# Interleaving two float32 tensors: eight equal tiles in place of seven and a shrinking tail

## The chip, the core and the metric

The kernel runs on one NeuronCore of one Trainium2 chip. The number that counts is the device time of one execution in microseconds (us), as the median of repeated runs. Beside it there is a profile of one execution, whose span runs from the first to the last instruction on the core and is therefore a little shorter than the device time.

## What is computed

Two inputs of the same shape are woven together element by element. Nothing is added or multiplied; every input element is read once and written once.

```python
batch, seq, dim = 32, 256, 1024
x, y: float32 [batch, seq, dim]

result = np.zeros((batch, seq, dim * 2), dtype=np.float32)
result[..., 0::2] = x
result[..., 1::2] = y
```

Each input has 8,388,608 elements, which is 33.55 MB. The kernel reads 67.11 MB and writes 67.11 MB.

## The kernel before

The tensors are taken as flat arrays. Spread over 128 partitions, each input is 65,536 elements for every partition. This is cut into tiles of `lw` elements per partition. A tile is one contiguous stretch of memory, and partition p holds its p-th row of `lw` elements. A full tile (`WL` = 8192) has rows of 32 KiB and is 4 MiB for x and 4 MiB for y.

```python
P = 128
WL = 8192
WS = 4096

xpool = ctx.enter_context(tc.tile_pool(name="xp", bufs=2))
ypool = ctx.enter_context(tc.tile_pool(name="yp", bufs=2))
opool = ctx.enter_context(tc.tile_pool(name="op", bufs=2))

lwidths = [WL] * (total // P // WL - 1) + [4096, 2048, 1024, 512, 512]

start = 0
for lw in lwidths:
    xtile = xpool.tile([P, WL], fp32, name="xtile")[:, :lw]
    ytile = ypool.tile([P, WL], fp32, name="ytile")[:, :lw]
    # ... xs, ys: 128 rows of lw elements, from element `start` on
    nc.sync.dma_start(out=xtile, in_=xs)                              # L49
    nc.sync.dma_start(out=ytile, in_=ys)                              # L50

    soff = 0
    while soff < lw:
        width = min(WS, lw - soff)
        otile = opool.tile([P, 2 * WS], fp32, name="otile")[:, : 2 * width]
        # ... os_: 128 rows of 2*width elements, 2*lw apart
        nc.vector.tensor_copy(out=otile[:, 0::2], in_=xsub)           # L63
        nc.vector.tensor_copy(out=otile[:, 1::2], in_=ysub)           # L64
        nc.scalar.dma_start(out=os_, in_=otile)                       # L65
        soff += width
    start += P * lw
```

Three engines take part. SyncE issues all loads on one DMA queue (q1 in the profile). VectorE (DVE) copies x into the even and y into the odd columns of an output tile. ScalarE (ACT) issues all stores on another DMA queue (q10).

A full tile is worked in two halves of 4096 elements. Each half gives one store of 128 rows of 32 KiB, so 4 MiB. In the text, "store (6,1)" means the second half of tile 6, where tiles are counted from 0. The tail consists of tiles of 4096, 2048, 1024, 512 and 512 elements, each worked in a single piece.

There are two buffers each for x tiles, y tiles and output tiles. Three waits follow from this:

- A load of tile i+2 is issued when the copies of tile i have read their buffer.
- The first copy of a half (L63) needs its x tile, and the output buffer of two halves earlier must have been stored.
- The second copy of a half (L64) needs its y tile.

Of the kernel before, what the change touches and what calls it, by code (L numbers as in the profile page):

```python
# [2 lines left out]

# [4 lines left out]


@with_exitstack
def kernel(
    ctx: ExitStack,
    tc: tile.TileContext,
    x: bass.AP,
    y: bass.AP,
    out: bass.AP,
):
    nc = tc.nc
    P = 128  # L20

    total = 1
    for s in x.shape:
        total *= s

    WL = 8192
    WS = 4096

    xf = x.rearrange("b s d -> (b s d)")
    yf = y.rearrange("b s d -> (b s d)")  # L30
    of = out.rearrange("b s d -> (b s d)")

    fp32 = mybir.dt.float32

    xpool = ctx.enter_context(tc.tile_pool(name="xp", bufs=2))
    ypool = ctx.enter_context(tc.tile_pool(name="yp", bufs=2))
    opool = ctx.enter_context(tc.tile_pool(name="op", bufs=2))

    lwidths = [WL] * (total // P // WL - 1) + [4096, 2048, 1024, 512, 512]
    assert sum(lwidths) == total // P  # L40

    start = 0
# [4 lines that stand above are left out]
        xs = dataclasses.replace(xf, offset=start, ap=[[lw, P], [1, lw]])  # L47
        ys = dataclasses.replace(yf, offset=start, ap=[[lw, P], [1, lw]])
# [7 lines that stand above are left out]
            os_ = dataclasses.replace(  # L56
                of,
                offset=2 * start + 2 * soff,
                ap=[[2 * lw, P], [1, 2 * width]],
            )  # L60
            xsub = xtile[:, soff : soff + width]
            ysub = ytile[:, soff : soff + width]
# [6 lines that stand above are left out]
    assert start == total  # L69


# [1 line left out]
_INS = ['x', 'y']  # L73
_OUTS = [((32, 256, 2048), 'float32')]


# [23 lines left out]
```

## Time and profile before

| quantity | value |
|---|---|
| device time, median of 3 runs | 318.54 us (318.42 to 318.84) |
| span of the profiled execution | 316.3 us |
| VectorE busy | 73.5 us, 38 copies |
| one copy of 128x4096 | 2.29 us (x30) |
| copies of 128x2048, 128x1024, 128x512 | 1.23, 0.70, 0.43 us (x2, x2, x4) |
| loads / stores issued | 24 / 19 |
| load of a full x tile, a full y tile, issue to landing (median) | 42.0, 59.2 us |
| store of 4 MiB, issue to landing (median) | 30.6 us |

The profile's page gives the busy time of each engine, the activity over 40 slices of the span, the traffic of the two DMA queues, and the chain of work that ended last. A transfer's time from issue to landing includes the time that it stands in its queue behind earlier transfers and the time in which the sixteen DMA engines serve the other queue. It is not what one transfer takes by itself. "Share" of the DMA is the mean busy share of the core's sixteen DMA engines. A transfer is made of packets, which the profile assigns to a window by their start; here a packet is one row of a tile, and there are also 4-byte packets that signal completion.

### The profile page before, as it was taken

How to read it: one execution, taken by the hardware profiler on the slowest of the kernel's cores; microseconds unless marked ns; L12 is line 12 of the kernel's file. 1: busy time of each engine (PE TensorE's matmuls, PEld its weight loads, DVE VectorE, ACT ScalarE, POOL GpSimd, SP SyncE). 2: the span in 40 equal slices, each digit the busy share in tenths (PEclk: the TensorE clock that was granted, in tenths of full speed). 3: DMA queues.
4: the chain of work that ended last, by engine and by line, in shares of the span. 5: the costliest groups of instructions: out<-in, count | busy, mean ns of one | idle time of the engine just before them, and what ended most of it. 6: DMA issues, size and time to landing. Idle time of an engine off the chain costs nothing.

```text
span 316.3 us, 179 instructions
## 1 busy us (share of the span) xinstructions
DVE 73.5 (23%) x38; POOL 0.2 (0%) x4
## 2 busy tenths in 40 slices
DVE  0334002214022220313205040050501414221022
POOL 0000000000000000000000000000000000000000
DMA  8999999999999999999999999999999999999997
GB/s 332 406 456 394 427 435 439 423 448 414 456 410 456 406 456 406 460 423 439 435 427 443 419 452 410 456 410 456 406 456 406 460 431 423 435 435 415 414 395 305
DMA packets 6192, 134.22 MB, mean 424 GB/s; under 512 B 688, under 2 KB 688, under 8 KB 1712
## 3 DMA queue, kind: packets, MB, share of 16 engines
q1 hardware_dynamic: 3456, 67.11, 49.9%
q10 hardware_dynamic: 2736, 67.11, 49.2%
HBM read 67.11 MB, written 67.11 MB: 424 GB/s over the span
## 4 chain that ended last, share of the span: by engine, by line
DMA 89%; DVE 10%; issue 0%; SPq 0%; DVEq 0%
DMA out_dram<-otile 59%; DMA ytile<-in_y_dram 29%; DVE otile L64 6%; DVE otile L63 4%; SPq L49 0%; DVEq L63 0%
## 5 line engine op out<-in xcount | busy, mean ns | idle before, releaser
L63 DVE COPY otile<-xtile 128x4096 f32<-128x4096 f32 (+3 forms) x19 | 37.1, 1958 | 203.7 <-DMA out_dram<-otile 180.6
L64 DVE COPY otile<-ytile 128x4096 f32<-128x4096 f32 (+3 forms) x19 | 37.1, 1956 | 35.5 <-DMA ytile<-in_y_dram 35.5
L84 POOL MEMSET const-bfloat16-1.0<- 128x1 bf16 x1 | 0.1, 103 | 0.0
L84 POOL MEMSET const-uint8-127<- 128x1 uint8 x1 | 0.1, 102 | 0.0
L84 POOL MEMSET const-float32-0.0<- 128x1 f32 x1 | 0.1, 99 | 0.2 <-issue 0.2
L84 POOL MEMSET const-float32-1.0<- 128x1 f32 x1 | 0.1, 99 | 0.0
## 6 DMA issues: line engine op xcount, KB each, us to landing
out_dram<-otile ACTq DMA_DIRECT2D x15, 4096.0 KB, 30.6
xtile<-in_x_dram SPq DMA_DIRECT2D x7, 4096.0 KB, 42.0
ytile<-in_y_dram SPq DMA_DIRECT2D x7, 4096.0 KB, 59.2
xtile<-in_x_dram SPq DMA_DIRECT2D x1, 2048.0 KB, 37.2
ytile<-in_y_dram SPq DMA_DIRECT2D x1, 2048.0 KB, 49.5
out_dram<-otile ACTq DMA_DIRECT2D x1, 2048.0 KB, 7.7
xtile<-in_x_dram SPq DMA_DIRECT2D x1, 1024.0 KB, 28.8
ytile<-in_y_dram SPq DMA_DIRECT2D x1, 1024.0 KB, 35.4
```

Source lines behind the costliest of these rows:

```text
L63: nc.vector.tensor_copy(out=otile[:, 0::2], in_=xsub)
L64: nc.vector.tensor_copy(out=otile[:, 1::2], in_=ysub)
L84: nc = _bacc.Bacc("TRN2", target_bir_lowering=False, num_devices=1)
```

## The change

The five tiles of decreasing size at the end are replaced by one more full tile. The total is the same 65,536 elements for each partition. All loads and all stores then are 4 MiB with rows of 32 KiB. There are 16 loads in place of 24, 16 stores in place of 19, and 32 copies in place of 38; everything up to the first seven tiles is issued in the same order. The purpose is a plainer kernel with only large transfers. What is given up is the gradual end, in which the last load, the last copies and the last store are all small.

```diff
--- before.py
+++ after.py
@@ -36,7 +36,7 @@
     ypool = ctx.enter_context(tc.tile_pool(name="yp", bufs=2))
     opool = ctx.enter_context(tc.tile_pool(name="op", bufs=2))
 
-    lwidths = [WL] * (total // P // WL - 1) + [4096, 2048, 1024, 512, 512]
+    lwidths = [WL] * (total // P // WL)
     assert sum(lwidths) == total // P
 
     start = 0
```

## The prediction

> **What bounds the kernel now.** I read first the page's slices and queue totals, then the stretches table by stage, then the DMA view of single windows, and last the timeline around the end. The page, with the busy tenths and the rates in the 40 slices:
>
> ```profile
> DVE 73.5 (23%) x38; POOL 0.2 (0%) x4
> ...
> DMA  8999999999999999999999999999999999999997
> GB/s 332 406 456 394 427 435 439 423 448 414 456 410 456 406 456 406 460 423 439 435 427 443 419 452 410 456 410 456 406 456 406 460 431 423 435 435 415 414 395 305
> ```
>
> VectorE works a quarter of the span. The DMA engines are full in every slice but the first and the last. The chain of waits gives 89% to DMA, but which transfer it names is of little use: both queues share the same sixteen engines, so a wait on a store is also a wait on loads. The kernel is a queue of 134.2 MB for a saturated resource. Only what keeps that resource idle, or makes it less efficient, costs time. The stretches by stage show where that is (duration, DVE busy, POOL busy, clock, DMA share, GB/s):
>
> ```profile
> 25.00:249.75 224.75, 50.02 (x23) 0.00 (x0) 1.00 1.00 431
> 249.75:301.00 51.25, 13.79 (x7) 0.00 (x0) 1.00 1.00 429
> 301.00:312.00 11.00, 2.30 (x6) 0.00 (x0) 1.00 0.98 397
> 312.00:316.30 4.30, 0.73 (x2) 0.00 (x0) 1.00 0.54 221
> ```
>
> Share 1.00 up to 301 us, through the body and the first tail tile; then 397 GB/s, and 221 in the last stretch. So a change of the tail can act only on the last 15 us, and, where packets are smaller, slightly before. The steady state is periodic; here is one period of the timeline (start, duration, operation, idle before and its releaser):
>
> ```profile
> 205.38 2.30 DVE L63 COPY otile<-xtile 128x4096 f32<-128x4096 f32 x1 [14.85 <-DMA out_dram<-otile]
> ...
> 211.03 2.30 DVE L64 COPY otile<-ytile 128x4096 f32<-128x4096 f32 x1 [3.35 <-DMA ytile<-in_y_dram]
> ...
> 224.75 2.30 DVE L63 COPY otile<-xtile 128x4096 f32<-128x4096 f32 x1 [11.43 <-DMA out_dram<-otile]
> ...
> 244.11 2.29 DVE L63 COPY otile<-xtile 128x4096 f32<-128x4096 f32 x1 [14.86 <-DMA out_dram<-otile]
> ...
> 249.75 2.30 DVE L64 COPY otile<-ytile 128x4096 f32<-128x4096 f32 x1 [3.35 <-DMA ytile<-in_y_dram]
> ```
>
> A tile takes 249.75 - 211.03 = 38.72 us and moves 16 MiB = 16.777 MB, so the full rate is 16.777 / 38.72 = 433.3 GB/s. That is the yardstick below. At 249.75 us tile 6's y has landed; what follows in the old kernel is the changed part.
>
> **What the Trainium skill says.** (1) "DMA: Bandwidth & Descriptors", section "Queues, rings and completion order": each DMA engine takes turns between the queues it has work for, a packet at a time. The trace agrees. With 32 KiB rows on both sides (100 to 138.7 us) the two queues have 50.2% and 50.0%; with stores of 32 KiB rows against loads of 16 KiB rows and less, the stores get two thirds (249.75 to 301 us):
>
> ```profile
> DMA packets 1343, 21.97 MB, mean 429 GB/s; under 512 B 144, under 2 KB 144, under 8 KB 383
> ## 3 DMA queue, kind: packets, MB, share of 16 engines
> q10 hardware_dynamic: 513, 14.71, 66.5%
> q1 hardware_dynamic: 830, 7.25, 33.4%
> ```
>
> (2) The same page, "Measured (HBM→SBUF, 128 partitions, SWDGE, issued from GpSimd)", asks for transfers of 1 MiB or more for 75% of the peak. The old tail has transfers of 256 and 512 KiB. The trace has them beside other transfers, and so loses much less: 397 GB/s from 301 to 312 us. (3) "HBM Reference", section "Specifications (TRN2)": 358 GB/s is a core's share of the memory, and a core alone gets about 425. The steady state here is 433.3, so the share does not bind in the mix of reads and writes. Whether it does when only writes are left is the rival below.
>
> **The change part by part.** The old tail has ten loads, five stores (the first of 4 MiB) and ten copies (two of them full-sized); the new tile has two loads, two stores and four copies, all full-sized. In VectorE time: out go 2 x 1.23 + 2 x 0.70 + 4 x 0.43 = 5.6 us, in come 2 x 2.29 = 4.6 us. None of that counts by itself, since VectorE idles beside full DMA engines.
>
> *Cost of the old tail.* From 249.75 to 301 us 21.97 MB were moved in 51.25 us; at 433.3 it would be 50.70, so 0.5 us is lost to smaller packets. From 301 us on, the DMA view counts 5.31 MB, which is 12.25 us of full rate. The last store is issued at 312.7 us (end of the last copy) and lands 2.6 us later, at 315.3 us, so 14.3 us pass: 2.0 us lost to short packets and to the end's waits (the two last 512-wide pieces each wait for a store before them: 5.79 and 2.29 us on VectorE). Together 2.5 us is all that the change can give.
>
> *New end by bytes.* After 249.75 us 21.97 + 5.31 = 27.28 MB remain to be started, and sixteen 32 KiB packets are under way, on average half done: 0.26 MB. At 433.3 GB/s, 27.54 MB take 63.6 us: 313.3 us as the mean end of the sixteen engines. They do not end together: the trace's completion records of tile 6's y run from 248.5 to 249.4 us. Taking 0.6 us for the last one beyond the mean gives a last landing at 313.9 us.
>
> *New end by the chain.* This asks whether the store queue ever runs dry. Tile 7's y copy starts one period after tile 6's, at 249.75 + 38.72 = 288.5 us. Store (6,0) lands for the copy at 244.11 + 38.72 = 282.8; store (6,1) would at 302.2 if loads still took every other turn. From 288.5 on there are none, and the remaining 13.7 us halve to 6.9: 295.4 us. Store (7,0) is issued when its y copy ends, 288.5 + 2.3 = 290.8, which is 4.6 us before (6,1) is through, so the queue does not run dry. A 4 MiB transfer alone takes 9.7 us (the first y lands 22.78 - 13.09 = 9.69 us after the first x, with nothing else running): 305.1 us. Store (7,1) needs the buffer of (6,1), free at 295.4, and two copies (4.5 us with their overlap): issued at 299.9, 5.2 us ahead. It lands at 305.1 + 9.7 = 314.8, less the 0.4 us that the copies' starts lie behind the landings: 314.4 us.
>
> The two ways give 313.9 and 314.4. In the old kernel the span ends 316.3 - 315.3 = 1.0 us after the last landing. So the new span is 314.9 to 315.4 us, 1.2 us under the old one in the middle; the time is 318.54 - 1.2 = 317.3 us, or 0.4% less.
>
> **The rivals.** *The exposed end.* The ordinary argument for shrinking tiles: after the last load lands, the old kernel has 316.3 - 308.9 = about 7 us left, the new one 315 - 288.5 = 26.5 us with nothing beside it but stores; one would fear up to 20 us. Against it: the bytes are the same, loads merely finish 20 us sooner because they get half of the turns to the end, where the old tail gave stores two thirds. As long as the store queue is full, nothing is lost. It would come true only if one of the two margins (4.6, 5.2 us) vanished; a dry spell costs at most 2 to 5 us: 319 to 322 us.
>
> *Stores alone are slower than the mix.* The last 26 us would be pure writing, a state the old trace nearly lacks. If writes got only the skill's 358 GB/s, (6,1)'s rest, (7,0) and (7,1), which is 26.3 us at 433.3, would take an estimated 31.8: +5.5 us, 322.8 us. Against it speaks the one stretch in which stores have the engines nearly to themselves, 304 to 308 us:
>
> ```profile
> DMA packets 192, 1.74 MB, mean 434 GB/s; under 512 B 16, under 2 KB 16, under 8 KB 96
> ## 3 DMA queue, kind: packets, MB, share of 16 engines
> q10 hardware_dynamic: 96, 1.57, 91.8%
> q1 hardware_dynamic: 96, 0.16, 10.7%
> ```
>
> Nine tenths stores at 434 GB/s. Loads alone (4 to 22 us, 99.5% of the engines' time on q1) move 430. I take it that one engine's pace on a packet is the limit, whatever the direction.
>
> *Nothing at all.* A last large store leaves the engines to finish apart, and the loss at the end replaces that of small packets: 318.0 to 318.6 us.
>
> **Range and chances.** 2.5 us is the most that can be won (316.0), and half of it is expected. The skew of the engines can take another 0.6 us or give it back. A somewhat slower pure store phase (5%) would add 1.3 us, which makes the range longer upwards: 316.6 to 318.8 us. A 2% gain (312.2) is out of reach, since the bytes at full rate forbid it: 0.01. A 2% loss (324.9) needs stores alone to be slower by a quarter: 0.03. Within 2%: 0.96.
>
> **What the changed profile should show.** The y copy of tile 7 at 288.5 us; the copy that waits for store (6,1) at 295.4, and thus the last store issued near 299.9; DMA share 1.00 from 25 us to about 313; a rate of 430 or more from 290 to 312 with q10 alone; last landing at 313.9 to 314.4; span near 315.1. I am wrong if the pure store stretch shows under 420 GB/s (second rival), or the share falls between 290 and 312 us (first), or the share is full and the span still no shorter (third).

## The result, and the profile after

The new kernel takes 316.74 us (median of 4 runs, 316.72 to 317.46) against 318.69 us of the old one beside it (4 runs). The ratio is 0.9939, with a 95% interval of 0.9914 to 0.9964. Run again in a later series it has 317.09 us and a ratio of 0.9940 (0.9928 to 0.9953). Predicted were 317.3 us and a range of 316.6 to 318.8, so the time lies close to the lower end. The span of the profiled execution is 315.0 us; 316.3 us was the old one, 314.9 to 315.4 the forecast.

The page of the new kernel, with the busy tenths and the rates in 40 slices:

```profile
DVE 72.6 (23%) x32; POOL 0.2 (0%) x4
...
DMA  8999999999999999999999999999999999999997
GB/s 333 408 458 387 412 454 412 454 412 454 412 454 412 458 408 458 408 458 408 458 408 458 424 441 424 441 429 437 429 437 429 437 429 437 433 433 437 429 437 304
```

The old kernel's rate fell over its last three slices (395 and 305 in the last two). Now only the last slice falls. The same stretches as before, from the table by stage (duration, DVE busy, POOL busy, clock, DMA share, GB/s):

```profile
25.00:249.75 224.75, 49.99 (x23) 0.00 (x0) 1.00 1.00 432
249.75:301.00 51.25, 15.88 (x7) 0.00 (x0) 1.00 1.00 434
301.00:312.00 11.00, 0.00 (x0) 0.00 (x0) 1.00 1.03 444
312.00:316.30 4.30, 0.00 (x0) 0.00 (x0) 1.00 0.09 38
```

Up to 249.75 us nothing has changed. From there to 312 us, where the old kernel had 429 and then 397 GB/s, the new one holds the full rate, and its last packet is done before 314 us. (A little over 433 in a short stretch comes from packets being counted where they start.) From 301 us on VectorE has nothing to do; from 288 us on only stores are left. The timeline of the last tile:

```profile
282.81 2.30 DVE L63 COPY otile<-xtile 128x4096 f32<-128x4096 f32 x1 [14.89 <-DMA out_dram<-otile]
288.48 2.30 DVE L64 COPY otile<-ytile 128x4096 f32<-128x4096 f32 x1 [3.38 <-DMA ytile<-in_y_dram]
294.90 2.29 DVE L63 COPY otile<-xtile 128x4096 f32<-128x4096 f32 x1 [4.12 <-DMA out_dram<-otile]
297.11 2.29 DVE L64 COPY otile<-ytile 128x4096 f32<-128x4096 f32 x1
```

The last store is issued at 297.11 + 2.29 = 299.4 us. The trace's completion records have store (7,0) through at 303.3 to 304.1 us and the last store at 313.0 to 313.8 us, depending on the DMA engine. So the store queue is never dry. Finally, what the DMA view shows from 302 to 308 us, when the stores are alone:

```profile
DMA packets 96, 2.62 MB, mean 437 GB/s; under 512 B 16, under 2 KB 16, under 8 KB 16
## 3 DMA queue, kind: packets, MB, share of 16 engines
q10 hardware_dynamic: 96, 2.62, 101.2%
```

### The profile page after: what moved, and what is told of

It reads as the page before. It is cut to its first block, busy times and chain, and to the rows that moved or that the text cites. A ratio compares the mean times of both kernels' runs of the same rounds, so it can differ in the third digit from the quotient of the medians.

```text
span 315.0 us, 148 instructions
## 1 busy us (share of the span) xinstructions
DVE 72.6 (23%) x32; POOL 0.2 (0%) x4
## 4 chain that ended last, share of the span: by engine, by line
DMA 83%; DVE 11%; DVEq 1%; issue 0%; SPq 0%
DMA out_dram<-otile 76%; DMA ytile<-in_y_dram 7%; DVE otile L64 6%; DVE otile L63 5%; DVEq L95 1%; SPq L49 0%; DVEq L63 0%
## 5 line engine op out<-in xcount | busy, mean ns | idle before, releaser
L63 DVE COPY otile<-xtile 128x4096 f32<-128x4096 f32 x16 | 36.6, 2294 | 197.9 <-DMA out_dram<-otile 184.8
L64 DVE COPY otile<-ytile 128x4096 f32<-128x4096 f32 x16 | 36.6, 2292 | 28.9 <-DMA ytile<-in_y_dram 28.9
```

## The experiments

Three questions were left. Which part of the old tail cost the time, its small packets or its waits? Was the end of the new kernel close to being exposed? And why had anyone needed a shrinking tail at all? Ratios are to the old kernel, timed beside each; spans are those of the profiled executions.

### The old tail with small buffers of its own

```diff
 (old kernel)
+    spool = ...tile_pool(name="sp", bufs=2);  spool1 = ...tile_pool(name="sp1", bufs=1)
     # both 512-wide tiles: xtile, ytile from spool
     # first 512-wide tile: otile from spool1
```

> Keeps every small transfer of the old tail, but gives the 512-wide tiles input buffers of their own and the first of them an output buffer of its own, so that the last loads and stores are queued early. My theory (the new kernel won about 0.7 us by having no small packets and about 1.0 us by having no dry spell after 301 us, and gave 0.3 us back because its engines finish apart): the dry spell goes, the small packets stay: span 315.3 to 315.6 us against 316.3 of the old and 315.0 of the new kernel, time ratio to the old kernel about 0.997. Rival 'only the waits at the end counted': 315.0 us or less. Rival 'only the size of the transfers counted': 316.2 to 316.4 us, ratio 1.000.

Measured: 317.79 us, ratio 0.9963 (0.9951 to 0.9975), span 315.8 us. From 301 to 312 us the rate is 417 GB/s where the old kernel had 397 and the new one 444, at the same DMA share of 0.98 as in the old kernel; some of the small packets now come before 301 us:

```profile
301.00:312.00 11.00, 2.06 (x4) 0.00 (x0) 1.00 0.98 417
```

Neither rival holds; the span is 0.2 us above the expected one. But the edit does not measure the waits, because it did not take them away. The copies changed their order (the first 512-wide piece now comes before the 2048-wide one), and VectorE still waits, for loads and for stores:

```profile
290.98 0.43 DVE L72 COPY osmall<-xsmall 128x512 f32<-128x512 f32 x1 [10.12 <-DMA xsmall<-in_x_dram]
304.98 0.70 DVE L72 COPY otile<-xtile 128x1024 f32<-128x1024 f32 x1 [10.64 <-DMA out_dram<-otile]
310.11 0.43 DVE L72 COPY otile<-xsmall 128x512 f32<-128x512 f32 x1 [3.83 <-DMA out_dram<-otile]
```

What changed is that the loads are through at 305.9 us in place of 311.9. The question is better answered from the packets themselves. A wait costs something only while the engines have no packet. Summed over a trace and divided by sixteen engines:

| kernel | packets, us | rest of the span, us | span, us |
|---|---|---|---|
| old | 313.4 | 2.9 | 316.3 |
| own_tail | 313.0 | 2.8 | 315.8 |
| new | 312.3 | 2.6 | 315.0 |

So 1.1 of the 1.35 us between the old and the new span are packet time, and 0.3 us are engines without a packet. Worked out from the median durations (next section), 0.7 of the 1.1 us are the small packets and 0.1 us the completion packets of the additional transfers. About 0.2 us are 2 KiB packets that take 145 to 267 ns in place of 84, near 302 us, just before the stores of the old kernel start again; own_tail does not have them. Most of the waits cost nothing, because the other queue filled the engines. What own_tail itself gains is less certain: 0.5 us in the profiled spans, but 1.0 us between the medians of all spans (316.8 and 315.8 us), and 0.37% of the 0.61% in time, both with wide intervals.

### What a packet costs

```diff
 (new kernel)
-    WL = 8192                    # rows16: 4096    rows8: 2048
-    WS = 4096                    # rows16: 2048    rows8: 1024
-    ... bufs=2 (three pools)     # rows16: 4       rows8: 8
```

> Sixteen equal tiles with 16 KiB rows for loads and stores, four buffers of half the size each: 64 transfers of 2 MiB in place of 32 of 4 MiB. My theory (cost per packet: a 16 KiB packet takes 611 ns in the trace against 1213 for 32 KiB, so 6 to 9 ns more per 32 KiB, 256 times for each engine, and 0.3 us of completion packets): 1.5 to 2.6 us more than the new kernel, less up to 0.5 us for a smaller end: span 316.2 to 317.6 us. Rival 'small transfers do not cost anything while the queue is full': 314.5 to 315.0 us.

> Thirty-two equal tiles with 8 KiB rows, eight buffers of a quarter of the size: 128 transfers of 1 MiB. My theory (8 KiB packets at 309 ns, four in place of one of 1213 ns: 14 to 23 ns more per 32 KiB, 256 times, and 0.9 us of completion packets): 4.4 to 6.8 us more than the new kernel, less up to 0.7 us at the end: span 318.7 to 321.8 us. Rival 'small transfers do not cost anything while the queue is full': 314.5 to 315.0 us.

Measured: rows16 318.47 us, ratio 0.9982 (0.9975 to 0.9989), span 316.7; rows8 321.72 us, ratio 1.0086 (1.0070 to 1.0102), span 319.8. Both lie in the expected ranges, 1.7 and 4.8 us above the new kernel. The stretch from 249.75 to 301 us, rows16 and then rows8, against 434 GB/s in the new kernel:

```profile
249.75:301.00 51.25, 12.58 (x11) 0.00 (x0) 1.00 1.01 430
```

```profile
249.75:301.00 51.25, 14.26 (x22) 0.00 (x0) 1.00 1.01 427
```

The DMA share is full in all three; the engines get less done in it. The packets' own durations in the old kernel's trace show a fixed part: 1213 ns for 32 KiB, 611 for 16, 309 for 8, 159 for 4 and 84 for 2 KiB (medians). Two halves take 7 to 9 ns more than the whole at every step. Sixteen packets of 2 KiB take 131 ns more than one of 32 KiB. It is a small price while the queue is full: transfers of 1 MiB (rows8) still run at 427 GB/s.

### Room at the end

```diff
 (new kernel, second half of tile 7 only; delay1: n = 2, delay4: n = 5)
-            nc.vector.tensor_copy(out=otile[:, 0::2], in_=xsub)
+            for _ in range(n):
+                nc.vector.tensor_copy(out=otile[:, 0::2], in_=xsub)
```

> The new kernel with the x copy of the very last half done twice (2.2 us more work on VectorE before the last store). In the new kernel's trace the last store is issued at 299.4 us and the store before it is through at 303.3 to 304.1 us. Theory (the end is bound by the store queue, the copies have room): issued at 301.6 us, still in time: span 314.9 to 315.2 us, unchanged. Rival 'the chain of copies at the end is exposed': 317.2 us.

> The same copy done five times (8.8 us more). Theory: the last store is issued at 308.2 us, after the queue has run dry at 303.3 to 304.1; with 1.0 us from issue to the first packet the engines stand for 5.1 to 5.9 us, and the span is 320.0 to 320.8 us. Rival 'the chain of copies at the end is exposed': the full 8.8 us, 323.8 us.

Measured: delay1 317.19 us, ratio 0.9937 (0.9921 to 0.9953), span 315.7, and 314.5 to 315.8 over its six runs. Delay4 323.09 us, ratio 1.0123 (1.0103 to 1.0142), span 320.8. In delay1 the last copy now starts later (the repeated x copy runs after the y copy):

```profile
300.03 2.29 DVE L65 COPY otile<-xtile 128x4096 f32<-128x4096 f32 x1
```

Its 2.2 us are free within the measurement: the ratio is that of the new kernel. The profiled span is 0.5 us above the forecast, and the trace shows no dry spell for it; what differs is that the engines finish the last store 1.4 us apart (313.1 to 314.5 us) instead of 0.8. In delay4, the stretches before, in and after the gap:

```profile
290.00:303.00 13.00, 8.40 (x5) 0.00 (x0) 1.00 1.00 434
303.00:310.00 7.00, 5.82 (x3) 0.00 (x0) 1.00 0.19 80
310.00:320.00 10.00, 0.00 (x0) 0.00 (x0) 1.00 0.86 367
```

From 303 to 310 us the DMA engines are 19% busy. The last store is issued at 308.9 us, 9.5 us later than in the new kernel; 5.8 us of that reach the span. Its first packet follows the issue by 0.8 us. In the new kernel the store before the last is through at 303.5 us (mean of the engines) and the last one is issued at 299.4, so the room was 303.5 - 299.4 - 0.8 = 3.3 us, where the prediction had 5.2. So the copies at the end count only once the store queue is dry.

### A half-sized last tile: the shrinking end again, with one step

```diff
 (new kernel)
-    lwidths = [WL] * (total // P // WL)
+    lwidths = [WL] * (total // P // WL - 1) + [4096, 4096]
```

> The new kernel with its last tile cut into two tiles of 4096 elements: 18 loads in place of 16, those of the last two tiles with 16 KiB rows; stores unchanged. My theory: the store queue stays full to the end, 16 KiB packets cost at most 10 ns per 32 KiB more (0.1 us in all): span 315.0 to 315.2 us, as the new kernel. Rival 'any shrinking of the end costs': 315.5 us or more. Rival 'an earlier end of the loads' share helps': under 314.7 us.

This missed by far: 320.68 us, ratio 1.0055 (1.0038 to 1.0072), span 318.5 us. No packet is smaller than 16 KiB, yet it is slower than the old tail. Its last copies, and the stretches around 304 us:

```profile
293.38 2.29 DVE L63 COPY otile<-xtile 128x4096 f32<-128x4096 f32 x1 [12.30 <-DMA xtile<-in_x_dram]
304.22 2.29 DVE L64 COPY otile<-ytile 128x4096 f32<-128x4096 f32 x1 [8.55 <-DMA ytile<-in_y_dram]
```

```profile
287.00:301.50 14.50, 2.29 (x1) 0.00 (x0) 1.00 1.01 434
301.50:307.50 6.00, 2.29 (x1) 0.00 (x0) 1.00 0.49 208
```

VectorE waits for the last x and the last y, not for a store. The last y lands at 303.9 us (288.1 in the new kernel). The stores issued by then are through at 302.0, and the next one can be issued only at 304.22 + 2.29 = 306.5 us: the engines stand idle for half of six microseconds. The loads are late because of the turns. This is the DMA view of two_halves from 255 to 300 us, stores above loads:

```profile
q10 hardware_dynamic: 440, 12.85, 66.1%
q1 hardware_dynamic: 448, 6.55, 34.0%
```

440 against 448 packets, of which some 48 each only signal completion: the queues alternate one for one. But a store's packet is 32 KiB and a load's now 16, so stores get two thirds of the engines, just when loads are what the end waits for. In the new kernel, both have 32 KiB and near half each.

### Evening the turns

```diff
 (two_halves)
 two_halves_even:   width = WS if start < 5 * P * WL else 2048
 two_halves_even4:  WS = 2048 throughout, opool bufs=4
 after_even4:       the new kernel with WS = 2048 throughout, opool bufs=4
```

> As two_halves, but from tile 5 on each store is 2048 elements wide and so has 16 KiB rows, as the loads of the two half tiles have. Theory from two_halves (the queues take turns packet by packet, stores of 32 KiB rows got two turns' worth against loads of 16 KiB rows, ran ahead, and the store queue then stood empty for 3.7 us waiting for the last load): with even rows the loads are not late, the dry spell goes, and about 0.5 us of smaller packets is added: span 315.2 to 315.8 us. Rival 'a half tile at the end costs by itself, by its chain of load, copy, store': stays at 318 us or more.

> two_halves once more, with all stores 2048 elements wide (16 KiB rows) and four output buffers of half the size in place of two, since two_halves_even starved its store queue in the middle for want of output buffers. Theory (packet turns: two_halves lost 3.7 us because stores with rows twice as long ran ahead of the loads): no dry spell, and 128 times 6 to 9 ns for the smaller store packets: span 315.7 to 316.4 us, within 0.3 us of after_even4. Rival 'half tiles at the end cost by themselves': 318.5 us or more.

> The control for two_halves_even4: the new kernel (eight full tiles) with the same 2048-wide stores and four output buffers. Theory: the new kernel's 315.0 us plus 0.8 to 1.1 us for the packets and 0.15 us for sixteen more completions, less up to 0.3 us at the end: span 315.7 to 316.2 us. If store packets of half the size cost nothing: 314.9 us.

Measured:

| kernel | time, us | ratio (95% interval) | span, us |
|---|---|---|---|
| two_halves_even | 320.11 | 1.0022 (1.0009 to 1.0035) | 318.7 |
| two_halves_even4 | 320.26 | 1.0044 (1.0030 to 1.0058) | 318.1 |
| after_even4 | 319.61 | 1.0021 (1.0012 to 1.0030) | 317.8 |

All three lie 1.6 to 2.9 us above the upper end of what was expected. Two_halves_even also varies most (spans of 316.5 to 319.5 us over 22 runs). Its end no longer waits for a load, but time is lost between 250 and 290 us instead:

```profile
250.00:270.00 20.00, 4.73 (x4) 0.00 (x0) 1.00 1.00 403
270.00:290.00 20.00, 7.09 (x6) 0.00 (x0) 1.00 0.99 396
```

The second expectation above puts this down to a want of output buffers. The trace does not show that: the DMA share is 1.00 and 0.99, so the engines are not short of work. The store queue is empty for only 2 us (282 to 284), with loads beside it. It is the load queue that runs empty (242 to 250 and 270 to 281 us), and where the loads start again, packets are slowed by 1.1 and 1.4 us of every engine's time.

In the pair that followed, half tiles cost 0.3 us of span (two_halves_even4 against after_even4; 0.65 us in the medians), against 3.5 us when store rows are longer than load rows (two_halves against the new kernel). That speaks for the turns and against the half tiles themselves. The pair is not a pure test, since its loads have the longer rows up to the half tiles and are far ahead by then. Rows16 comes closer: its last tiles are half tiles too, its rows are 16 KiB on both sides throughout, and the engines stay full to 312 us, although VectorE waits 6.3 us for the last y:

```profile
301.00:312.00 11.00, 1.88 (x2) 0.00 (x0) 1.00 1.00 429
```

Why after_even4 is slow was not foreseen. The loads, whose rows are now the longer ones, run ahead until all input buffers are full, and their queue empties. From 118 to 124 us the DMA view has stores alone; then the loads start again, and the stretch from 124 to 132 us drops to 395 GB/s at full share:

```profile
118.00:124.00 6.00, 4.69 (x5) 0.00 (x0) 1.00 1.01 431
124.00:132.00 8.00, 1.23 (x1) 0.00 (x0) 1.00 1.01 395
200.00:207.00 7.00, 2.89 (x3) 0.00 (x0) 1.00 1.03 403
207.00:213.00 6.00, 0.00 (x0) 0.00 (x0) 1.00 1.01 404
```

The same again at 200 us. Over the whole trace the packets take 3.3 us more of every engine's time than in the new kernel; 2.0 us of that are slowed packets, the rest smaller ones. Yet the loads start again beside stores five times, and only at 126 and 205 us are packets slowed. At 87, 165 and 244 us none is; here are the first and the last of these:

```profile
86.50:94.00 7.50, 1.23 (x1) 0.00 (x0) 1.00 1.01 435
244.20:251.00 6.80, 1.23 (x1) 0.00 (x0) 1.00 1.01 436
```

With rows of equal length, in the new kernel and in rows16, neither queue stands empty for longer than 1.5 us before its end; with longer rows on one side, that side ran into a buffer wait.

### The loss at the first store

```diff
 (new kernel; y0_act: n = 1, y01_act: n = 2)
-        nc.sync.dma_start(out=ytile, in_=ys)
+        (nc.scalar if start < n * P * WL else nc.sync).dma_start(out=ytile, in_=ys)
```

> The new kernel with only the first y load issued by ScalarE in place of SyncE, so that both queues start at once. In both kernels' traces some 0.8 us of the engines' time is lost near 28 us, just as the first store comes up on ScalarE's queue. If that is the cost of the queue's first use, it is now paid beside the start: span 314.2 to 314.6 us. If it belongs to the first writes to memory, nothing changes: 314.8 to 315.2 us.

> The new kernel with the first two y loads on ScalarE's queue, so that this queue is never empty between its start and the first store. The traces show packets slowed by 0.8 us of every engine's time (1.2 us in y0_act) whenever a queue that is empty starts while the other is busy. Theory (the cost belongs to the start of an empty queue beside a busy one): the loss near 28 us disappears: span 313.9 to 314.5 us against 315.0 to 315.3 of the new kernel. Rival 'the cost belongs to the first writes to memory': it only moves to the first store, near 41 us, and the span stays at 314.9 to 315.5 us.

Measured: y0_act 316.81 us, ratio 0.9928 (0.9914 to 0.9941), span 315.0; y01_act 318.36 us, ratio 0.9980 (0.9970 to 0.9991), span 316.7. Y0_act is not to be told from the new kernel. Its slowed packets still come at 28 us. The span of y01_act missed both forecasts. The loss at 28 us is gone, but slowed packets stand at 39 to 45 us, where the first store now follows the loads on a queue that was never empty. That contradicts my theory of the empty queue, and is what the rival had forecast for this place. But y01_act also shows slowed packets at 87 to 94 us, some 1.5 us of every engine's time, where the loads' queue had run empty (last landing 81.0 us) and started again beside stores, and nothing is written for the first time. So the first writes alone don't explain it either. What these cases have in common is the change from traffic in one direction to traffic in both. That was not tested, and it is not enough: three of the five such changes in after_even4 slow nothing.

### The new kernel again

> The new kernel unchanged, beside the two others on the same chip. Span 314.5 to 315.8 us, ratio to the old kernel 0.992 to 0.996.

317.09 us, ratio 0.9940 (0.9928 to 0.9953), spans 315.1 to 315.5 us: as expected. No kernel of the series is clearly faster than this one.

## Why the prediction was right, point by point

- **"A queue of 134.2 MB for a saturated resource": right.** Share and rate are unchanged up to 249.75 us, and VectorE's 0.9 us less work plays no part: delay1 adds 2.2 us to it at the end without a change in time.
- **"2.5 us is all that the change can give", of which about half arrives: right (1.35 us of span).** The kind was less right. The prediction placed 2.0 of the 2.5 us in "short packets and the end's waits" without dividing them. The packets turn out to be 1.1 us of the gain and the idle engines 0.3; the waits of 5.79 and 2.29 us on VectorE hardly count.
- **New end by bytes, 313.3 us in the mean and 313.9 for the last engine: right.** The records run from 313.0 to 313.8 us, with a mean of 313.2.
- **New end by the chain, 314.4 us: 0.6 us late.** The y copy came at 288.48 (288.5 forecast), the copy after store (6,1) at 294.90 (295.4), the last issue at 299.4 (299.9). The y load is through at 287.2 to 288.1 us, somewhat before the copy starts, and the step counted the freed turns from the copy.
- **The two margins, 4.6 and 5.2 us: real, but the second too large.** It was 3.3 us. Store (7,0) is through by 303.5 us in the mean, not 305.1, and a store's first packet comes 0.8 us after its issue.
- **"So the new span is 314.9 to 315.4 us": right (315.0), with a slip.** The 1.0 us after the last landing was counted from 315.3 us, where the semaphore tells of it, but added to forecasts made from completion records. These end at 315.0 us in the old kernel, which leaves 1.3 us; in the new one it is 1.2. The later end by the chain hid the slip.
- **"The time is 318.54 - 1.2": the mis-sized term.** It took device time minus span to be the same in both kernels. It is 318.49 - 316.3 = 2.2 us in the old one and 316.73 - 315.0 = 1.7 in the new one. That is most of the difference between 317.3 and 316.74, and it means that 0.45 of the 1.95 us gained lie outside the span, where the profile shows nothing. That the time still fell into the range is owed to the range's width. The difference goes with the program: runs of the old kernel and of delay4 have about 2.2 us, own_tail and the two even4 kernels 1.9 to 2.2, all others 1.7 to 1.9. Why stays open.
- **The exposed end: refuted here, and true next door.** With 3.3 us of room the new kernel is clear of it. (The old kernel's last load lands at 312.3 us, not at 308.9, so 4 us followed it and not 7.) Two_halves shows it at full size, 3.5 us, and shows what the prediction had noted without drawing the conclusion, that the old tail gave stores two thirds. A half tile makes the loads' packets smaller than the stores' before them, so the last loads come late. In the old kernel, too, the store queue stands empty, from 298.5 to 302.7 us, but there the loads of the later pieces keep the engines 91% busy. That its further steps were needed for this was not tested.
- **Stores alone slower: refuted.** They ran at 437 GB/s from 302 to 308 us, the mix at 433.

## What to carry to other kernels

When the DMA engines are full to the end, a shrinking tail has nothing to hide: the bytes set the time, and the tail adds packet time (1.1 us of 316 here) and a little idling (0.3 us). Where two queues take turns packet by packet, as here, the length of a row decides who gets the engines (66% against 34% in two_halves). So keep the rows of loads and stores alike, or the side with the shorter rows arrives late and the other runs dry. Before cutting the end finer, look at whether the queue that ends last ever runs empty, and how long before that its next transfer is issued.

## What the hardware showed that was not expected

- Where traffic in one direction becomes traffic in both, time can be lost although the engines stay busy: single packets of 32 KiB then take 1.3 to 2.6 us in place of 1.21. In the new kernel this is some 0.8 us of every engine's time between 26 and 31 us. All the slowed packets there are loads, and nearly all start before the first store's packets do, at 29.8 us. After_even4 loses as much at 126 us, and 1.1 us at 205, but nothing in three other places of the same kind. The way back, from both to stores alone, at 288 us, shows no such packets. Neither the empty queue nor the first writes alone explain it; the cause is open.
- A transfer's sixteen engines finish up to 3.3 us apart (store records in after_even4; 0.8 us at the new kernel's end, 1.4 in delay1, 0.1 in delay4). The last engine ends the span, so such differences at the end move it by some tenths of a microsecond.
